# ScalarE's instructions ordered by the framework's scheduler instead of by the program

## The chip, the core and the metric

The kernel runs on one core of one Trainium2 chip, in one launch. The core has five engines, each with an instruction queue of its own: TensorE (PE in the profile; its weight loads are PEld), VectorE (DVE), ScalarE (ACT), GpSimd (POOL) and SyncE (SP), which here issues the transfers from and to the device's memory (HBM). The engines wait for one another by semaphores. The metric is the device time of the core in microseconds (us): 2713.55, the median of three runs (2711.83, 2713.55 and 2714.47).

## The reference

The computation is in float32 on one sequence of 512 tokens with 2048 channels. First come two hybrid attention layers:

```python
h = rms_norm(x, pre_w);  proj = h @ w_in                      # 2048 -> 5952
y_a = diff_attention(...)             # 4 heads, two softmaxes, their difference, causal
y_b = sliding_window_attention(...)   # 16 heads of 64, window 128, sinks
y_c = causal_attention(...)           # 4 heads; q and k, v from rms-normed latents of 512
y = concat(y_a, y_b, y_c) * silu(gates);  x = x + rms_norm(y @ w_out, post_w)
```

Then a second block: rmsnorm, a projection to mixer inputs and gates, of which 1024 channels go through a pooling mixer (trailing means over windows of 2, 4, 8 and 16 tokens, then a 256x256 map per group) and 1024 through a state space mixer (64 groups, 64 complex states each, a GLU behind), the gates, an output projection, a gated per-layer embedding and the norms around them.

## The kernel before

**Projections.** Each float32 operand is split in two float32r halves, and a product is three matmuls (`mm3`): high by high, low by high, high by low. The activations of a projection stand split in one big tile `B` (high and low halves of 16 k-tiles of 128 channels). Weights stream. SyncE loads a piece of up to 128x1024 into `wraw`, a ring of 3. For each unit of up to 128x512, ScalarE casts or scales it into `whi` (a ring of 6, `WBUFS`) and VectorE forms `wlo`, the rest; `split_unit` writes both, and `prefetch` has SyncE issue the next load once a `wlo` is written. `ahead` keeps 4 units split beside the one in use. A `whi` may be written only when its `wraw` has landed, and when TensorE and VectorE have used up the tile that had its place in the ring six units before. Results gather in PSUM banks: four of tag `pp`, two of `t`, one each of `s0` and `s1`. ScalarE and VectorE copy or combine them into tiles in SBUF (`raw`, `craw`, `o`, `gt`, `g`), which frees the bank.

**Norms.** `norm_list` takes a token tile of 128 rows through its steps: four squares with a sum (ScalarE, `junk<-x`), a reciprocal root in ten small VectorE instructions (`ry`), four scalings `h`, 16 transposes on TensorE into a bank, and `transpose_to_B`: a ScalarE cast to the high half of `B` and a VectorE subtraction for the low. `first_norm` does this at the start of the kernel for token tiles 0 and 1; ScalarE scales two of the `h` there. Tiles 2 and 3 are loaded then, too, but their steps run later, beside the first projection.

**Other work.** Attention, rotations, the pooling means, the state space scan and the gates are closures that run between the steps of the projections. `gate` has ScalarE write tanh of a bank to `g`, and VectorE multiply it in, which frees the bank. `split` is a ScalarE cast `hi` and a VectorE `lo`.

**What sets the order.** The program writes the instructions of all engines in one sequence, by a rough account of its own (`Model`, `chain`, `tick`) of when each engine would get to them. All are issued through one helper, so all rows of the profile carry its line, L166. `run` writes them inside a block that makes every engine keep the order in which they were written:

```python
        with self.tc.manual_schedule():
            self.first_norm(t["x"])
```

Each engine runs its queue in that order, and one that waits holds up all behind it. Slots of the tile pools are handed out as the program is laid out, in order.

Of the kernel before, what the change touches and what calls it, by code (L numbers as in the profile page):

```python
# [85 lines left out]
class Model:  # L86
    """A rough account, kept while the program is written, of when each engine gets to an instruction and
    each tile is written. Work beside the projections is placed where its operands should be there."""
# [53 lines left out]
    def ready(self, need, eng, banks):  # L142
        """Whether eng would find these tiles written and banks of these tags free."""
        limit = max(self.t[eng], self.t["PE"])
        for tag in set(banks):
            names, bufs = self.held.get(tag, ()), self.bufs.get(tag, 1)
            for i in range(len(names) + banks.count(tag) - bufs):
                if self.used.get(names[i], 0.0) + 130 > limit:
                    return False
        return all(x is not None and self.done.get(x.tensor.name, 1e18) + 130 <= limit for x in need)  # L150
# [5 lines left out]
class Engine:  # L156
    """An engine's instructions, passed on and entered in the model."""
# [24 lines left out]
class Step:  # L182
    """A piece of work that is best begun when eng would find the tiles that need() names written."""
# [9 lines left out]
class K:  # L193
# [87 lines left out]
    def chain(self, fs, gap=1.0, delay=0.0, q=None):  # L281
        """Steps that run one after another, at least gap ticks apart; None leaves a place free, and one
        that returns False is called again later."""
        self.n += 1
        heapq.heappush(self.bg if q is None else q, (self.now + delay + gap, self.n, list(fs), gap))

    def force(self, q):
        """Runs the next step that can be, ready or not."""
        self.run_urgent()
        late, got = [], False  # L290
        while q and not got:
            x = heapq.heappop(q)
            got = self.is_emitted(x[2][0]) and self.run_step(x[2][0]) is not False
            if got:
                self.advance(q, x)
            else:
                late.append(x)
        assert got
        for x in late:
            heapq.heappush(q, x)  # L300
# [17 lines left out]
    def att_start(self, units, ticks, delay=0, done=None):  # L318
        """Units of (scores, exp, norm, transposes, values); one is begun every so many ticks."""
        gap = ticks / len(units)  # L320
        t = self.now + delay
        for x in units:
            self.queue.append([list(x), 0, t])
            t += gap
        if done:
            self.queue[-1][0].append(done)

    def run_units(self, force=False):
        """A unit goes on once the one before it is two parts further."""
        before = 5  # L330
        for x in list(self.queue):
            steps, pos, t = x
            if t > self.now and not force:
                break
            while pos < len(steps) and (before >= min(pos + 2, 5)):
                f = steps[pos]
                if not (self.is_emitted(f) if force else self.is_ready(f)):
                    break
                self.run_step(f)
                pos += 1  # L340
                if force:
                    force = False
                    x[1] = pos
                    if pos == len(steps):
                        self.queue.remove(x)
                    return True
            x[1] = pos
            if pos == len(steps):
                self.queue.remove(x)
                before = 5  # L350
            else:
                before = pos
        return False
# [18 lines left out]
    def rsqrt_list(self, out, ss, scale, eps, n):  # L372
        """Closures that put (ss * scale + eps) ** -0.5 into out[0]."""
        nc = self.nc
        st = {}

        def first():
            mk = (lambda x: self.small(n, F32, x)) if n <= 8 else (lambda x: self.u(F32, [P, n], x))
            st["v"], st["y"], st["w"] = mk("rv"), mk("ry"), mk("rw")
            v, y = st["v"], st["y"]  # L380
            out.append(y)
            nc.vector.tensor_scalar(out=v, in0=ss, scalar1=scale, scalar2=eps, op0=ALU.mult, op1=ALU.add)
            nc.vector.tensor_scalar(out=y.bitcast(I32), in0=v.bitcast(I32), scalar1=-0.5, scalar2=1597463007.0,
                                    op0=ALU.mult, op1=ALU.add)

        def it():
            v, y, w = st["v"], st["y"], st["w"]
            nc.vector.scalar_tensor_tensor(out=w, in0=y, scalar=-0.5, in1=y, op0=ALU.mult, op1=ALU.mult)
            nc.vector.tensor_tensor(out=w, in0=w, in1=v, op=ALU.mult)
            nc.vector.scalar_tensor_tensor(out=y, in0=w, scalar=1.5, in1=y, op0=ALU.add, op1=ALU.mult)  # L390

        return [first, it, it, it]
# [7 lines left out]
    def rsqrt1(self, ss, scale, eps):  # L400
        """(ss * scale + eps) ** -0.5 of one column; the powers of two that the steps leave are taken out at the end."""
# [18 lines left out]
    def units(self, name):  # L420
        """How many units of up to 512 columns, and the k-tiles and columns of each."""
# [10 lines left out]
    def plan_loads(self):  # L432
        """Pieces of one or two units, and after which split the load of each is issued."""
# [55 lines left out]
    def ahead(self, n=AHEAD):  # L489
        """Keeps n units of the ring split beside the one in use."""  # L490
# [20 lines left out]
    def proj_cm(self, name, mov, ncol, evac, hook=None):  # L511
        """out[channel, token]: the weights stationary."""
# [17 lines left out]
    def proj_tm(self, name, stat, ms, evac, hook=None):  # L530
        """out[token, channel]: the activations stationary."""
# [99 lines left out]
    def reduce_list(self, tiles):  # L631
        """The steps of reduce_angle as closures."""
        return [lambda x=x: self.reduce_angle(*tiles(), part=x) for x in range(4)]

    def reduce_angle(self, a, k, r, part=None):
        """r = a - 2 pi round(a / 2 pi), the multiple taken off in pieces that are exact; in one go or by part."""
# [48 lines left out]
    def norm_list(self, m, xt, after_sq=None, tags="tttt", act=False, first=False):  # L685
        """Closures: x / rms(x), transposed into the columns of token tile m of B."""
# [72 lines left out]
    def rope_lists(self, raws, fins):  # L759
        """Rotates the [channel, token] tiles; fins get each result."""  # L760
# [29 lines left out]
    def to_stack(self, dst, i, keys=False):  # L790
        """Two heads of 64 rows for products whose 128 rows carry both parts: [hi; lo] and [lo; hi] of them, or,
        for keys, [hi; hi] of either, and the two heads' lo."""
# [14 lines left out]
    def mm_stacked(self, outs, qs, ks, rows, start=True):  # L807
        """hi hi + lo hi over 128 rows, then hi lo over the head's own 64."""
# [117 lines left out]
    def da_units(self, l, h, qk, va, done):  # L926
        """qk() gives the tiles of q and k; done(o) comes after the last one."""
# [3 lines left out]
        units = []  # L931
# [91 lines left out]
    def cm_norm_list(self, xs, n, eps, cols, after):  # L1023
        """Closures: x * rsqrt(mean over the channels) * column, for [channel, token] tiles, in place."""
# [60 lines left out]
    def plan_tail(self, name, last):  # L1085
        """The last chunk stays on the chip, split; the end of it stays in the ring."""
# [6 lines left out]
    def layer(self, l):  # L1093
# [66 lines left out]
        # sliding window  # L1160
# [44 lines left out]
        # differential attention  # L1205
# [47 lines left out]
        # latent attention, over the last projection and the first chunk of the output projection  # L1253
# [25 lines left out]
        def hook(k0):  # L1279
            """Rows of B that the last projection has passed take the branches' outputs."""  # L1280
# [27 lines left out]
    def tail_rows(self, name, evac):  # L1308
        """The resident last chunk, token tile by token tile."""
# [70 lines left out]
    def cmul(self, dst, a, b, e1, e2, tmp, neg_im=False):  # L1380
        """dst = a * b for (re, im) pairs of views; tmp: two scratch views."""
# [12 lines left out]
    def exp_list(self, get):  # L1394
        """exp of get() = (x, out, k, t), in closures; x, k and t are overwritten."""
# [157 lines left out]
    def cdiag(self, c, pr):  # L1553
        """c of two groups, each in its rows and columns."""
        return self.cd[c][pr // 16][:, pr % 16].rearrange("p e c -> p (e c)")

    def ssm_lists(self, ct, ud, yd, put):
        """Closures of one channel tile (8 groups): its tables, then the scan and its output."""
# [226 lines left out]
    def second(self, xsrc):  # L1785
# [36 lines left out]
        # pooling branch  # L1822
# [84 lines left out]
        # gated linear unit of the state space branch  # L1907
# [29 lines left out]
        # output projection, residual  # L1937
# [49 lines left out]
        # embedding, its gate, final norm  # L1987
# [56 lines left out]
    def run(self, upto=99):  # L2044
# [7 lines left out]
        with self.tc.manual_schedule():  # L2052
# [16 lines left out]
def _layout(inp):  # L2069
# [80 lines left out]
    # constants of the shapes  # L2150
# [35 lines left out]
```

## Time and profile before

| | |
|---|---|
| median of three runs | 2713.55 us (2711.83 to 2714.47) |
| span of the profiled execution, its own time in the profile | 2711.1 us |
| TensorE busy | 2648.9 us (98%) |
| VectorE busy | 1599.1 us (59%) |
| ScalarE busy | 1197.8 us (44%) |
| GpSimd busy | 415.5 us (15%) |
| mean granted TensorE clock | 0.993 of full speed |
| mean traffic of the DMA queues | 114 GB/s |

The profile is of one execution. Its page gives the busy time of each engine; a timeline gives for each instruction, or run of like instructions (x2, x4), the start, the time they took, what is written from what, and in brackets how long the engine had stood idle just before and what released it. Tiles go by the program's names with the buffer numbers left out. TensorE stands idle for 2711.1 - 2648.9 = 62.2 us in all. The largest pieces are 10.0 us before its first instruction and waits of up to 5.7 us for VectorE.

### The profile page before, as it was taken

The numbers are of one execution on the slowest core, as the hardware profiler recorded it, in microseconds if no ns is written. First come the engines' busy times: TensorE is split into PE (matmuls) and PEld (weight loads), VectorE is DVE, ScalarE is ACT, GpSimd is POOL, SyncE is SP. The second block draws the span as 40 slices with busy tenths as digits, with TensorE's granted clock in tenths as the row PEclk, the third lists the DMA queues.
The fourth block names the chain that finished last, engine by engine and source line by source line (L and its number), as shares of the span: only waits on it lengthen the run. The fifth ranks groups of instructions, "written<-read, shape, count | busy, mean of one in ns | idle before, by whom it ended". The sixth has DMA issues, their size and how long they took to land. (4 is left out here: it accounts for less than half of the span.)

```text
span 2711.1 us, 36803 instructions
## 1 busy us (share of the span) xinstructions
PE 2648.9 (98%) x13120; PEld 2201.1 (81%) x13120; DVE 1599.1 (59%) x3247; ACT 1197.8 (44%) x2543; POOL 415.5 (15%) x822
## 2 busy tenths in 40 slices
PE   8999999999999999999999999989999999999998
PEld 8978888877888887888777788888877888888886
DVE  6785566675624758546667562486767654333344
ACT  7565444544434646444444443463333343232341
POOL 0100001100001110000110000117777800000000
PEclk9999999999999999999999999999999999999999
DMA  6642333223235553224422323454232332352332
GB/s 213 186 120 86 91 119 113 75 78 125 71 116 163 173 147 94 94 89 122 117 71 79 124 70 117 160 186 141 84 94 82 100 99 94 118 164 69 101 127 91
DMA packets 125831, 309.04 MB, mean 114 GB/s; under 512 B 33616, under 2 KB 34512, under 8 KB 125648
## 3 DMA queue, kind: packets, MB, share of 16 engines
q1 hardware_dynamic: 125648, 306.69, 36.1%
q8 instruction: 103, 1.69, 0.3%
q14 instruction: 80, 0.66, 0.1%
HBM read 264.68 MB, written 20.97 MB: 105 GB/s over the span
## 5 line engine op out<-in xcount | busy, mean ns | idle before, releaser
L166 PE MATMUL pp<-B,whi 128*128 128x512 f32 (+1 forms) x4256 | 1222.6, 373 | 7.5 <-DVE g L166 6.2
L166 PEld LDWEIGHTS pp<-B,whi 128*128 128x128 f32 x4256 | 753.9, 190 | 137.7 <-issue 7.1
L166 PE MATMUL pp<-B,wlo 128*128 128x512 f32 (+1 forms) x2128 | 782.4, 368 | 8.9 <-DVE wlo L166 8.9
L166 PE MATMUL pp<-whi,B 128*128 128x512 f32 x1984 | 626.0, 391 | 1.6 <-ACT raw L166 1.0
L166 DVE SCALAR_TENSOR_TENSOR wlo<-wraw,p_cols,whi 128x512 fp32r<-128x512 f32 (+1 forms) x576 | 448.4, 795 | 293.7 <-ACT whi L166 290.0
L166 ACT ACTIVATE whi<-wraw,p_cols 128x512 fp32r<-128x512 f32 (+1 forms) x576 | 395.9, 713 | 206.8 <-PE pp L166 170.8
L166 PEld LDWEIGHTS pp<-B,wlo 128*128 128x128 f32 x2128 | 403.5, 190 | 78.2 <-DVE wlo L166 10.3
L166 PEld LDWEIGHTS pp<-whi,B 128*128 128x128 f32 x1984 | 372.4, 188 | 82.2 <-ACT raw L166 1.8
L166 DVE TENSOR_TENSOR wlo<-wraw,whi 128x512 fp32r<-128x512 f32 x288 | 197.8, 696 | 386.9 <-ACT whi L166 386.5
L166 PE MATMUL pp<-wlo,B 128*128 128x512 f32 x992 | 386.2, 389 | 0.0
L166 ACT CAST whi<-wraw 128x512 fp32r<-128x512 f32 x288 | 175.5, 623 | 323.4 <-PE pp L166 311.0
L166 PEld LDWEIGHTS pp<-wlo,B 128*128 128x128 f32 x992 | 186.4, 188 | 37.1
L166 POOL TENSOR_TENSOR sw<-sw,sinT 128x512 f32<-128x512 f32 x40 | 55.2, 1386 | 764.7 <-DMA sw<-raw 708.8
L166 POOL TENSOR_TENSOR o<-o,x 128x512 f32<-128x512 f32 x32 | 51.1, 1623 | 378.4 <-DVE o L166 370.4
L166 PE MATMUL pp<-rh,B 128*128 128x512 f32 x320 | 103.1, 392 | 0.0
L166 PE MATMUL pp<-hi,whi 128*128 128x512 f32 x224 | 88.3, 394 | 1.4 <-DVE lo L166 1.4
L166 PE MATMUL pp<-hi,wlo 128*128 128x512 f32 x224 | 87.3, 390 | 0.0
L166 PE MATMUL pp<-lo,whi 128*128 128x512 f32 x224 | 87.3, 390 | 0.0
L166 ACT ACTIVATE p<-p,nb 128x256 f32<-128x256 f32 (+1 forms) x128 | 60.2, 473 | 57.9 <-DVE nb L166 57.8
L166 ACT CAST pth<-t 128x256 fp32r<-128x256 f32 (+1 forms) x96 | 29.2, 339 | 113.2 <-PE t L166 110.5
L166 PEld LDWEIGHTS pp<-rh,B 128*128 128x128 f32 x320 | 60.1, 188 | 12.3
L166 DVE TENSOR_SCALAR p<-p,sm 128x128 f32<-128x128 f32 (+1 forms) x192 | 66.0, 386 | 4.1 <-DVE sm L166 0.5
(257 smaller groups left out, 3162.7 us busy)
## 6 DMA issues: line engine op xcount, KB each, us to landing
wraw<-in_w SPq DMA_DIRECT2D x426, 512.0 KB, 3.5
sw<-raw SPq DMA_DIRECT2D x160, 64.0 KB, 2.0
wraw<-in_w SPq DMA_DIRECT2D x24, 384.0 KB, 3.2
x<-in_x SPq DMA_DIRECT2D x32, 256.0 KB, 5.2
x<-o SPq DMA_DIRECT2D x32, 256.0 KB, 2.6
ybd<-yb SPq DMA_DIRECT2D x16, 256.0 KB, 4.5
yb<-ybd SPq DMA_DIRECT2D x16, 256.0 KB, 3.8
x<-x SPq DMA_DIRECT2D x16, 256.0 KB, 4.4
```

The costliest lines, as they stand in the source:

```text
L166: r = f(*a, **k)
```

## The change

The block that holds the order is given the engines that it is to hold: TensorE, SyncE, GpSimd and VectorE. ScalarE is no longer among them; its instructions are put in order by the framework's scheduler when the program is built, among those that its own account has ready. The rest of the diff blanks comments and docstrings:

```diff
@@ -140,7 +140,7 @@
     def ready(self, need, eng, banks):
-        """Whether eng would find these tiles written and banks of these tags free."""
+
...
@@ -2049,7 +2049,8 @@
             self.plan_layer(l)
         self.plan_second()
         self.plan_loads()
-        with self.tc.manual_schedule():
+        ordered = {mybir.EngineType.PE, mybir.EngineType.SP, mybir.EngineType.Pool, mybir.EngineType.DVE}
+        with self.tc.manual_schedule(engines=ordered):
             self.first_norm(t["x"])
```

In the built program the orders of TensorE, VectorE, GpSimd and SyncE are as before. On ScalarE the same compute instructions stand in another order over the whole program (2438 lines of difference for some 2080 rows); table loads are 5 in both. Three places follow; in each row stand the line, the operation, what is written from what, and the shape.

At the start of the program, ScalarE before: `x_102` is the last piece of token tile 1; `pp`, `s` and `t` are banks with transposes of token tiles 0 and 1; `h_215` and `h_217` are the two scalings that ScalarE has there.

```order
L166 ACTIVATE junk,s_146<-x_102 128x512
L166 CAST B<-pp_187 128x4x128
L166 CAST B<-pp_193 128x4x128
L166 CAST B<-pp_199 128x4x128
L166 CAST B<-pp_205 128x4x128
L166 ACTIVATE h_215<-x_101,ry_176 128x512
L166 ACTIVATE h_217<-x_102,ry_176 128x512
L166 ACTIVATE whi_223<-wraw_111,p_cols 128x384
L166 CAST B<-s_226 128x4x128
L166 CAST B<-s_234 128x4x128
L166 CAST B<-t_241 128x4x128
L166 CAST B<-t_248 128x4x128
```

The last square of tile 1 is followed by the casts of tile 0, and the two `h` before the first `whi`. On the same engine now, from the sixth `whi` of the program on (`x_107` to `x_110` are token tile 2, `x_121` to `x_124` token tile 3):

```order
L166 ACTIVATE whi_286<-wraw_115,p_cols 128x384
L166 ACTIVATE junk,s_330<-x_107 128x512
L166 ACTIVATE junk,s_330<-x_108 128x512
L166 ACTIVATE junk,s_330<-x_109 128x512
L166 ACTIVATE junk,s_330<-x_110 128x512
L166 ACTIVATE junk,s_623<-x_121 128x512
L166 ACTIVATE junk,s_623<-x_122 128x512
L166 ACTIVATE junk,s_623<-x_123 128x512
L166 ACTIVATE junk,s_623<-x_124 128x512
L166 CAST B<-pp_187 128x4x128
L166 CAST B<-pp_193 128x4x128
L166 CAST B<-pp_199 128x4x128
```

Six `whi` (five more stand before this piece) and the eight squares of tiles 2 and 3 now stand between the square of `x_102` and the casts; `h_215` follows the cast from `pp_199`, then the cast from `pp_205`, then `h_217`.

At the pooling gates of the second block (2116 to 2128 us in the profile), the difference on ScalarE, - before and + now. `mt` are copies for the state space mixer, `g` the tanh of four finished banks:

```order
-L166 CAST whi4240_20631<-wraw4207_20478 128x512
 L166 COPY mt4243_20653<-t4245_20655 128x4x64
 L166 COPY mt4244_20654<-t4245_20655 128x4x64
-L166 ACTIVATE whi4246_20662<-wraw4222_20546,p_cols_97 128x512
 L166 COPY mt4243_20653<-t4248_20678 128x4x64
 L166 COPY mt4244_20654<-t4248_20678 128x4x64
-L166 ACTIVATE whi4249_20685<-wraw4222_20546,p_cols_97 128x512
 L166 ACTIVATE g4251_20691<-pp4147_20141 128x512
 L166 ACTIVATE g4252_20697<-pp4148_20142 128x512
 L166 ACTIVATE g4256_20712<-pp4149_20143 128x512
 L166 ACTIVATE g4257_20718<-pp4150_20144 128x512
+L166 CAST whi4240_20631<-wraw4207_20478 128x512
```

The cast `whi4240` moved from ahead of the `mt` copies to behind the four `g`, and `whi4246` and `whi4249` follow it there. On VectorE the order is unchanged: the `wlo` of `whi4240`, two `lb`, two `ht`, the `wlo` of `whi4246`, then the first product with `g4251`.

In layer 0, at 333 us in the profile, the difference on ScalarE around two casts `hi` of softmax rows in banks `t`; `yb` are copies of attention outputs, `sa` and `sb` casts of rotated queries:

```order
+L166 ACTIVATE whi750_3659<-wraw712_3501,p_cols_97 128x512
+L166 ACTIVATE whi757_3696<-wraw712_3501,p_cols_97 128x512
+L166 ACTIVATE whi760_3717<-wraw727_3562,p_cols_97 128x512
 L166 CAST hi745_3648<-t744_3643 128x512
 L166 CAST hi748_3656<-t747_3651 128x512
-L166 ACTIVATE whi750_3659<-wraw712_3501,p_cols_97 128x512
 L166 COPY yb543_2638<-t752_3679 64x128 x2
 L166 COPY yb544_2639<-t752_3679 64x128 x2
 L166 CAST sa753_3691<-raw725_3554 128x512
 L166 CAST sb754_3692<-raw725_3554 64x512
-L166 ACTIVATE whi757_3696<-wraw712_3501,p_cols_97 128x512
-L166 ACTIVATE whi760_3717<-wraw727_3562,p_cols_97 128x512
```

Three `whi` moved ahead of the casts `hi745` and `hi748`; the first had stood just behind them, the other two behind the `yb`, `sa` and `sb`.

## Rows read from the trace of the kernel before

**Rows 1.** The page's head and its part 1: busy us, share of span, instructions

```profile
span 2711.1 us, 36803 instructions
PE 2648.9 (98%) x13120; PEld 2201.1 (81%) x13120; DVE 1599.1 (59%) x3247; ACT 1197.8 (44%) x2543; POOL 415.5 (15%) x822
```

**Rows 2.** Waits of ScalarE, VectorE, TensorE: us in total, times, longest

```profile
ACT whi L166 <- PE pp L166: 481.8, 281, 10.8
...
DVE wlo L166 <- ACT whi L166: 676.4, 373, 7.9
...
PE pp L166 <- DVE wlo L166: 8.9, 6, 2.4
...
PE t L166 <- DVE p L166: 5.0, 5, 1.8
```

**Rows 3.** SyncE's timeline at the start, and the loads issued from 7.4 us

```profile
7.44 6.70 SPq L166 DMA_DIRECT2D x<-in_x  x8
...
x<-in_x SPq DMA_DIRECT2D x8, 256.0 KB, 6.0
```

**Rows 4.** ScalarE's timeline, 11.5 to 30 us: start, us, instruction, [idle before]

```profile
11.96 1.54 ACT L166 CAST B<-pp 128x512 fp32r<-128x512 f32 x3
...
14.19 1.33 ACT L166 ACTIVATE h<-x,ry 128x512 f32<-128x512 f32 x2
...
25.28 0.62 ACT L166 ACTIVATE junk<-x 128x512 bf16<-128x512 f32 x1
...
26.02 0.63 ACT L166 ACTIVATE junk<-x 128x512 bf16<-128x512 f32 x1
```

**Rows 5.** TensorE's timeline at the start

```profile
16.50 1.92 PE L166 MATMUL t<-c_ident,h 128*128 128x128 f32 x8
18.06 1.17 PE L166 MATMUL pp<-B,whi 128*128 128x256 f32 x2
```

**Rows 6.** ScalarE's timeline at the pooling gate

```profile
2116.43 0.62 ACT L166 CAST whi<-wraw 128x512 fp32r<-128x512 f32 x1
...
2125.32 2.21 ACT L166 ACTIVATE g<-pp 128x512 f32<-128x512 f32 x4
```

**Rows 7.** VectorE's timeline at the pooling gate

```profile
2117.78 1.29 DVE L166 TENSOR_TENSOR lb<-lb,lbt 128x512 f32<-128x512 f32 x2
...
2122.26 0.75 DVE L166 SCALAR_TENSOR_TENSOR wlo<-wraw,p_cols,whi 128x512 fp32r<-128x512 f32 x1 [1.98 <-ACT whi L166]
2125.95 1.28 DVE L166 SCALAR_TENSOR_TENSOR g<-g,pp 128x512 f32<-128x512 f32 x2 [2.94 <-ACT g L166]
...
2132.67 1.24 DVE L166 SCALAR_TENSOR_TENSOR wlo<-wraw,p_cols,whi 128x512 fp32r<-128x512 f32 x1
```

**Rows 8.** TensorE's timeline at the pooling gate

```profile
2126.74 0.46 PE L166 MATMUL pp<-hi,whi 128*128 128x512 f32 x1
```

**Rows 9.** Timelines: ScalarE at 333, TensorE at 336, ScalarE at 1750 us

```profile
332.98 1.08 ACT L166 CAST hi<-t 128x512 fp32r<-128x512 f32 x2 [3.20 <-PE t L166]
...
335.96 0.39 PE L166 MATMUL t<-hi,v 128*128 128x512 f32 x1
...
1749.65 2.56 ACT L166 ACTIVATE h<-o,ry 128x512 f32<-128x512 f32 x4 [0.90 <-DVE ry L166]
```

**Rows 10.** Timelines: GpSimd at 1944, VectorE at 1946, TensorE at 2004 us

```profile
1944.20 1.19 POOL L166 TENSOR_TENSOR pw<-pv 128x511 f32<-128x511 f32 x1 [2.43 <-ACT hi L166]
...
1946.05 0.69 DVE L166 SCALAR_TENSOR_TENSOR pw<-pw,pv 128x512 f32<-128x512 f32 x1
...
2003.74 1.22 PE L166 MATMUL pp<-B,whi 128*128 128x512 f32 x2 [5.71 <-DVE g L166]
```

**Rows 11.** Timelines around 540 us: TensorE, VectorE

```profile
544.90 0.66 PE L166 MATMUL t<-c_ident,p 128*128 128x128 f32 x4 [1.68 <-DVE p L166]
...
540.00 1.28 DVE L166 SCALAR_TENSOR_TENSOR wlo<-wraw,p_cols,whi 128x512 fp32r<-128x512 f32 x1 [2.12 <-ACT whi L166]
```

**Rows 12.** A stretch: us, busy of five engines (PE, PEld, ...), granted clock, DMA

```profile
2002.30:2009.10 6.80, 5.36 (x21) 4.98 (x22) 6.25 (x13) 0.00 (x0) 3.08 (x3) 0.50 0.28 85
```

## The prediction

> **What bounds the kernel now.** I read the page first, then the waits of three engines, then the timelines of the places where ScalarE's order changes. TensorE is busy 2648.9 of 2711.1 us, ScalarE 44% [rows 1]. So the time is TensorE's work and some 62 us in which it stands still, and a new order on ScalarE can only move those 62 us, or add to them. ScalarE has much idle time, and the reason is the ring of weights: 281 times, 481.8 us in all, a `whi` is the next instruction and waits until TensorE has used a tile of the ring up; VectorE in turn stands 676.4 us waiting for `whi` before it can make `wlo` [rows 2]. TensorE waits little for the outcome, 8.9 us for `wlo` and 5.0 us for the softmax rows `p` [rows 2]. A reader should take two things from this. A `whi` that may not start yet is the usual state of ScalarE's queue, so whatever stands behind one waits for TensorE; and a `whi` earlier by some us gives VectorE its idle time back, which matters where VectorE is late.
>
> The profiled execution has no other time than its span, 2711.1 us, which is 2.45 us (0.09%) below the median of the runs, 2713.55. I sum changes of the span and add 2.45.
>
> **The change, part by part.** No instruction is added, removed or resized, and the program order of TensorE, VectorE, GpSimd and SyncE stays. ScalarE's instructions are the same; where they stand is new. The cost is therefore found place by place: does an instruction that TensorE needs now stand behind one that becomes ready later?
>
> *Start.* Before, ScalarE begins the 4 `B` casts at 11.96 us, the two `h` of 0.66 us each at 14.19 [rows 4]. Now six `whi` and the eight squares of token tiles 2 and 3 stand ahead of them, as the first two fences of the change show. Those squares need x tiles that are not there yet: SyncE issues the eight loads from 7.44 to 14.14 us, so the last begins at about 13.3, and a load takes 6.0 us to land [rows 3]; that is 19.3 to 20.1. The last square takes 0.74 more (25.28 to 26.02 is one with its sum [rows 4]). So the first cast goes at 20.0 to 20.9 instead of 11.96. Behind it come three casts (1.54 us), `h`, a cast (0.51) and `h`: the second `h` ends at 23.4 to 24.3. TensorE needs it for four transposes (8 take from 16.50 to 18.06, 0.2 us each) and then begins the first projection [rows 5]: 24.2 to 25.1 instead of 18.06. That is +6.1 to +7.0; I take **+6.6**. VectorE cannot help, since its halves of `B` follow the casts one by one. The six `whi` cost nothing here, they run while the loads are still on their way. In what ScalarE no longer does later there is no gain, since it idles there.
>
> *The pooling gate.* Before, the `whi` of 2116.43 us stood well ahead of the four tanh `g` of 2125.32 [rows 6]. Now it and two more stand behind all four (third fence), and those are tied to TensorE: the last `g` ends at 2127.53. `whi` is then ready at about 2128.1, eleven us late. VectorE keeps its order and stops at the `wlo` of that unit, which stands ahead of `lb` at 2117.78; behind that `wlo` (0.67) are two `lb` and two `ht` (1.22 each pair), then the `wlo` of 2122.26 (0.67), and only then `g`, which before began at 2125.95 [rows 7]. So 2128.1 + 0.6 + 2.4 + 0.7 = 2131.8, and the first `g` frees its bank at 2132.4. TensorE began the next product in that bank at 2126.74, without idle time [rows 8]. It stands until 2132.5: **+5.8**. Bounds: not under 3, as the `whi`, the `wlo` and the `g` alone are that long; at most 5.8 and four VectorE instructions stretched like the `wlo` of 2132.67, which took 1.24 in place of 0.75 us beside GpSimd [rows 7], so 7.8.
> The Trainium skill (SBUF — State Buffer, "Who interferes with whom") says that a VectorE instruction with two SBUF inputs and a GpSimd instruction that reads SBUF exclude each other, one fully waiting. By that rule the four `lb` and `ht` would each wait for a GpSimd instruction and the place would cost about 8; the rows are divided, the 1.24 agrees and the `lb` of 0.65 each do not, and I stay with the rows.
>
> *A cast or scaling behind a `whi` that must wait.* At 332.98 us two `hi` casts feed TensorE's `t<-hi,v` at 335.96 [rows 9]. Now two `whi` that were far behind stand ahead (fourth fence); the second needs the ring's tile that TensorE gives back as it ends the unit before 335.96. So `hi` starts after 336.0 + 0.7, the first product waits until 337.3, and `lo` comes later still: **+2.0**. Its twin in layer 1 costs **+1.6** by the same count. At the ends of both layers one square (0.74) or one `whi` (0.6) is put ahead of the `h` scalings that TensorE's transposes follow directly, as at 1749.65 [rows 9]; six such places at about 0.8 make **+4.8**. Five more before 170 us, `raw` copies and `B` casts behind a `whi`, I put at **+3.4** together. The four add to 11.8; nothing if `whi` turns out to be ready each time, 18 if waits pile up.
>
> *GpSimd.* Tiles are handed out in another order, and GpSimd's `pw` at 1944.20 now gets its tile only when VectorE has ended the `pw` of 1946.05, at 1946.74. GpSimd could go no earlier than 1944.2 before, so it is 2.5 us late and works without a pause to the place where TensorE waits 5.71 us, at 2003.74 [rows 10]; 0.6 of it has room. **+1.9**, between 0 and 2.5.
>
> *Gains.* At 544.90 TensorE waits 1.68 us for `p`, and VectorE had stood 2.12 us before 540.00 for a `whi` that ScalarE made late [rows 11]. With `whi` ahead the `wlo` falls into that idle time, and the gap closes, 1.7 here and in its twin. Eight smaller gaps of this kind give 0.2 to 1.0 each, 3.7 together. Sum **-7.1**, at most the 13.9 us that TensorE waits for `wlo` and `p` [rows 2].
>
> *Clock.* Around the wait that ends at 2003.74 the granted clock is 0.50 (1.2 instead of 2.4 GHz) for 6.8 us, with 5.36 us of work in them [rows 12]; that work would take half as long at full clock, so such a wait costs 2.7 us more than itself. I add **+2.7** at the pooling gate, where the new idle time is as long (0 to 3.4), and **+2.0** at the start, where the clock had just risen (0 to 3.4).
>
> Sum: 6.6 + 5.8 + 11.8 + 1.9 + 4.7 - 7.1 = +23.7. Span 2734.8, time **2737 us**.
>
> **The rivals.** (a) *Earlier `whi` wins.* The scheduler's preference for `whi` feeds VectorE earlier everywhere, and the small places cost nothing since `whi` is ready in time. For it: VectorE's 676 us of waiting [rows 2]. Price: the start with its clock (+8.6) against -13.9: 2708 us. It decides where the gain passes the start's 8.6, so only if the pooling gate, too, is hidden. Against it: `g` there has no room, TensorE followed it without idle time [rows 8]. Chance 0.07, faster in most of it.
>
> (b) *It makes no difference that can be measured* (within 0.2%, 5.4 us): ScalarE is 44% busy and TensorE runs ahead, the places that I count have more room than I see, only start and gate remain partly and the gains pay them: 6.6 + 3 - 7.1 = +2.5, 2716 us. Against it: the start's loads land when they land. The Trainium skill (Trace Analysis, "Identifying Performance Opportunities") has improvement come from the most-contended engine; by it an order on an engine at 44% would be near this case. Chance 0.10.
>
> (c) *Waits pile up.* Each place that stops TensorE shifts the rest, the clock halves at several more of them, and VectorE and GpSimd meet. Upper ends: 7.0 + 7.8 + 18 + 2.5 + 6.8 - 4 = +38, 2752 us; with what I have not seen in some hundred further moved `whi`, 2765. Chance 0.13.
>
> (d) The forecast, the sum of places within 2720 to 2750: 0.70.
>
> The range goes from 2717 (part of b) to 2756 (most of c). Faster takes most of (a), 0.06; within 0.2% takes (b) and the rest of (a), 0.11; slower takes (c) and (d), 0.83. A change of 0.2% is about what a measurement of this kernel tells from none.
>
> **What would show it.** In the profile after: the first `CAST B<-pp` near 21 us instead of 11.96, behind squares; the first projection near 24.7. Around 2132 us a wait of TensorE of 5 to 8 us on VectorE's `g` that was not there, with a stretch of half clock behind it. `hi` behind `whi` near 340 and TensorE waiting for `hi` or `lo`. No wait for `p` near 551. TensorE's busy time grows by no more than the half clock makes of it. The prediction is wrong if the first projection begins before 20 us, if no new wait over 3 us stands at the gate, or if TensorE's total wait falls.

## The result and the profile after

The changed kernel takes 2730.7 us (median of four runs, 2727.2 to 2732.2) against 2712.7 us for the kernel before (four runs, 2708.2 to 2714.5): ratio 1.0066, 95% interval 1.0054 to 1.0078. It is slower by 18 us; 2737 were forecast.

The page's head of the kernel after:

```profile
span 2727.9 us, 36907 instructions
PE 2650.2 (97%) x13120; PEld 2201.5 (81%) x13120; DVE 1581.5 (58%) x3247; ACT 1218.5 (45%) x2543; POOL 419.2 (15%) x822
```

TensorE's busy time grew by 1.3 us only, and the span by 16.8 [rows 1]. So the loss is standing still. TensorE's waits that changed most, first in the kernel before, then in the kernel after, and behind them the two waits of the ring (us in total, times, longest):

```profile
PE pp L166 <- DVE g L166: 6.2, 2, 5.7
...
PE s L166 <- DVE ys L166: 4.7, 1, 4.7
PE t L166 <- ACT h L166: 3.3, 3, 2.2
```

```profile
PE t L166 <- ACT h L166: 14.8, 7, 7.6
PE pp L166 <- DVE g L166: 12.6, 3, 6.5
...
PE pp L166 <- DVE wlo L166: 7.7, 7, 2.3
PE pp L166 <- ACT raw L166: 6.5, 7, 3.0
...
PE t L166 <- DVE p L166: 2.2, 4, 0.8
...
PE s L166 <- DVE ys L166: 0.7, 1, 0.7
...
ACT whi L166 <- PE pp L166: 837.4, 492, 10.8
...
DVE wlo L166 <- ACT whi L166: 527.0, 295, 7.5
```

The wait of VectorE for `whi` fell from 676.4 to 527.0 us, that of ScalarE for TensorE rose from 481.8 to 837.4 [rows 2]: ScalarE makes `whi` as early as the ring lets it, and stands in front of the next one, with whatever is behind it. The price is in TensorE's waits for `h` (14.8 instead of 3.3, of which 7.6 at the start) and for `g` (12.6 instead of 6.2); the gain is in `p`, 2.2 instead of 5.0 [rows 2], and in `ys`, 0.7 instead of 4.7.

Since TensorE runs the same instructions in the same order, the start of each can be subtracted, after minus before; where that difference steps, a place costs or gives. The steps, worked out so from the two traces, in the order of the prediction's terms (a step holds the wait and what a lower clock takes behind it):

| place (us in the kernel before) | forecast | measured step |
|---|---|---|
| start, 16 to 21 | +6.6 and +2.0 | +6.65 |
| pooling gate, 2127 | +5.8 and +2.7 | +7.5 |
| `hi` at 336 and its twin at 1216 | +2.0, +1.6 | +3.9, +1.65 |
| six layer-end places, 883 to 1812 | +4.8 | +9.8 (926: 4.4, 1805: 2.7) |
| five places before 170 | +3.4 | +6.2 (135 to 141: 4.1) |
| GpSimd's `pw`, felt at 2004 | +1.9 | -0.1 |
| gains for `p` and the like (489, 545, 760, 1078, 1370, 1424, 2607) | -7.1 | -8.5 |
| losses not foreseen (406, 419, 983, 1029) | | +3.1 |
| gains not foreseen (910, 1050, 1507, 1782 to 1797, 2103) | | -13.6 |

A trace is of one execution, and some steps come and go between traces whose order at the place is the same: 1.6 us where a lower clock follows a wait or does not (138, 336, 627, 1507, 1791), up to 2.5 us at the start, and at places behind a load 3.5 to 4.4 us (926) and 1.0 to 4.6 us (1805). So the table is good to a few us in a row with such a place.

**The start** [rows 4, 5]. ScalarE, then TensorE, in the kernel after:

```profile
11.82 3.14 ACT L166 ACTIVATE whi<-wraw,p_cols 128x384 fp32r<-128x384 f32 x6 [0.18 <-DMA wraw<-in_w]
14.87 0.61 ACT L166 ACTIVATE junk<-x 128x512 bf16<-128x512 f32 x1
...
20.19 0.63 ACT L166 ACTIVATE junk<-x 128x512 bf16<-128x512 f32 x1
...
20.82 1.54 ACT L166 CAST B<-pp 128x512 fp32r<-128x512 f32 x3
...
23.33 0.75 ACT L166 ACTIVATE h<-x,ry 128x512 f32<-128x512 f32 x1
...
23.03 2.21 PE L166 MATMUL t<-c_ident,h 128*128 128x128 f32 x8 [7.62 <-ACT h L166]
24.90 1.05 PE L166 MATMUL pp<-B,whi 128*128 128x256 f32 x2
```

The six `whi` run from 11.82, the eight squares from 14.87, one every 0.75 us, the last at 20.19, and the first cast goes at 20.82 instead of 11.96. The second `h` is begun at 23.33, and the first projection starts at 24.90 instead of 18.06; 20.0 to 20.9, 23.4 to 24.3 (its end) and 24.2 to 25.1 were forecast.

The times are those forecast, the reason is another. By the trace the eight x tiles land between 14.34 and 19.49 us, each ahead of its square: only the second square stands for its tile, 0.09 us, and the last begins 0.7 us after its own has landed. What fills the stretch is ScalarE's own work, 9.0 us from the first `whi` to the first cast. In the traces of three of the experiments below (e2, e7 and e8), with the same order at the start, it is 8.9 us, and no square waits.

**The pooling gate** [rows 6 to 8]. ScalarE, VectorE and TensorE in the kernel after:

```profile
2135.59 2.67 ACT L166 ACTIVATE g<-pp 128x512 f32<-128x512 f32 x4
2138.16 0.61 ACT L166 CAST whi<-wraw 128x512 fp32r<-128x512 f32 x1
...
2138.80 0.69 DVE L166 TENSOR_TENSOR wlo<-wraw,whi 128x512 fp32r<-128x512 f32 x1 [7.55 <-ACT whi L166]
2139.41 1.29 DVE L166 TENSOR_TENSOR lb<-lb,lbt 128x512 f32<-128x512 f32 x2
...
2142.49 1.27 DVE L166 SCALAR_TENSOR_TENSOR g<-g,pp 128x512 f32<-128x512 f32 x2
...
2143.21 0.79 PE L166 MATMUL pp<-hi,whi 128*128 128x512 f32 x1 [5.59 <-DVE g L166]
```

The stretch behind it (columns as in rows 12):

```profile
2143.20:2147.00 3.80, 3.79 (x11) 3.10 (x12) 3.26 (x6) 0.00 (x0) 3.72 (x8) 0.50 0.40 132
```

The `whi` follows the four `g` at 2138.16, VectorE had stood 7.55 us for it, `g` is begun at 2142.49, and TensorE, which before did not wait here, stands 5.59 us (5.8 forecast). Behind that it has 0.50 of its clock. The four `lb` and `ht` between are not stretched (1.29 for two).

**`hi` behind `whi`** [rows 9]. ScalarE and TensorE in the kernel after, then the stretch behind:

```profile
349.29 0.72 ACT L166 ACTIVATE whi<-wraw,p_cols 128x512 fp32r<-128x512 f32 x1 [2.88 <-PE pp L166]
349.92 1.05 ACT L166 CAST hi<-t 128x512 fp32r<-128x512 f32 x2
...
351.26 0.53 PE L166 MATMUL t<-hi,v 128*128 128x512 f32 x1 [2.06 <-DVE lo L166]
```

```profile
352.00:356.00 4.00, 4.00 (x13) 3.13 (x12) 2.38 (x4) 1.96 (x6) 0.25 (x1) 0.62 0.08 34
```

Both `hi` are cast at 349.92, at once behind the `whi` that had waited for TensorE, and TensorE waits 2.06 us for `lo`, where 2.0 were forecast. Not forecast: the granted clock is 0.62 on average in the 4 us behind, which is most of the other 1.9 us of the step.

**A load that has not landed.** At the largest of the layer-end places the `whi` waits for something else. ScalarE and TensorE in the kernel after (926 us in the kernel before):

```profile
937.33 0.72 ACT L166 ACTIVATE whi<-wraw,p_cols 128x512 fp32r<-128x512 f32 x1 [3.32 <-DMA wraw<-in_w]
937.96 0.57 ACT L166 CAST B<-t 128x512 fp32r<-128x512 f32 x1
...
941.84 0.92 ACT L166 COPY raw<-pp 128x256 f32<-128x256 f32 x3
...
942.26 0.80 PE L166 MATMUL pp<-B,whi 128*128 128x256 f32 x2 [3.01 <-ACT raw L166]
```

A `whi` stands 3.32 us for its `wraw`, with a cast of `B` and the `raw` copies behind it, and TensorE waits 3.01 us for `raw` to free a bank. I had counted `whi` that wait for TensorE, 0.8 us a place; a load can be later than that. How late differs from run to run: this load took 7.3 us from issue to landing, in the trace of the experiment e1 (same order here) 5.7 us, and TensorE's wait was 2.0 there.

**The gains** [rows 11]. VectorE and TensorE at the place of the wait for `p` in the kernel after:

```profile
554.58 1.41 DVE L166 SCALAR_TENSOR_TENSOR wlo<-wraw,p_cols,whi 128x512 fp32r<-128x512 f32 x2
...
560.56 0.60 PE L166 MATMUL t<-c_ident,p 128*128 128x128 f32 x4
```

The two `wlo` begin at 554.58, some 3 us earlier against TensorE than at 540.00 before, in the time in which VectorE used to stand for `whi`; `p` comes before TensorE needs it, and TensorE's transposes have no idle time in front.

**The largest unforeseen gain** is at 2103 us. VectorE, GpSimd and TensorE there in the kernel before, then the same instructions in the kernel after:

```profile
2096.45 5.06 DVE L166 TENSOR_TENSOR sp<-sx,z 64x252 f32<-64x252 f32 x4
...
2097.70 2.35 POOL L166 TENSOR_TENSOR lbt<-pk,sbb 128x512 f32<-128x512 f32 x2
...
2102.97 1.20 PE L166 MATMUL s<-sp,ht 128*128 128x128 f32 x4 [4.67 <-DVE ys L166]
```

```profile
2111.05 2.54 DVE L166 TENSOR_TENSOR sp<-sx,z 64x252 f32<-64x252 f32 x4
...
2113.68 3.12 POOL L166 TENSOR_TENSOR lbt<-pk,sbb 128x512 f32<-128x512 f32 x2 [1.32 <-DVE sp L166]
...
2115.07 0.68 PE L166 MATMUL s<-sp,ht 128*128 128x128 f32 x4 [0.71 <-DVE ys L166]
```

Before, four `sp` took 5.06 us, the first beside GpSimd's `pw`, the others beside its `lbt`, and TensorE waited 4.67 us for the `ys` behind them. After, GpSimd waits for `sp` before it begins `lbt`: in the program the wait for the slot that the tile of `lbt` is given is now for VectorE, where it was for TensorE. The four `sp` take 2.54 us (1.25 of them the first, again beside `pw`) and TensorE waits 0.71. A new order on ScalarE changed when tiles come free, with that the slots that later tiles get, and with that whom GpSimd waits for.

### The profile page after: what moved, and what is told of

Its sections match the earlier page's. It is cut to its first block, busy times and chain, and to the rows that moved or that the text cites. A ratio compares the mean times of both kernels' runs of the same rounds, so it can differ in the third digit from the quotient of the medians.

```text
span 2727.9 us, 36907 instructions
## 1 busy us (share of the span) xinstructions
PE 2650.2 (97%) x13120; PEld 2201.5 (81%) x13120; DVE 1581.5 (58%) x3247; ACT 1218.5 (45%) x2543; POOL 419.2 (15%) x822
## 3 DMA queue, kind: packets, MB, share of 16 engines
q8 instruction: 103, 1.69, 0.3%
## 5 line engine op out<-in xcount | busy, mean ns | idle before, releaser
L166 ACT ACTIVATE whi<-wraw,p_cols 128x512 fp32r<-128x512 f32 (+1 forms) x576 | 406.8, 714 | 552.4 <-PE pp L166 436.8
L166 DVE TENSOR_TENSOR p<-s,c_mask 128x512 f32<-128x512 f32 (+1 forms) x64 | 39.5, 618 | 69.8 <-PE s L166 69.7
L166 DVE TENSOR_TENSOR s<-s,c_mask 128x128 f32<-128x128 f32 x96 | 28.3, 295 | 72.3 <-PE s L166 72.1
```

The source lines that it names most:

```text
L166: r = f(*a, **k)
```

## The experiments

There are eight, e1 to e8. In all but e4, ScalarE's order is the program's in some stretches and the scheduler's in the others; a stretch is named by weight units, counted by `split_unit`. All other engines keep the program's order. With no free stretch this gives the order of the kernel before, with one over the whole program that of the kernel after. The edit to the kernel after, for the first:

```diff
         def call(*a, **k):
-            r = f(*a, **k)
+            r = f(*a, **k); model.keep(name, r)
...
+    FREE = ((12, 10000),)
+
+    def keep(self, eng, r):
+        if eng != "ACT":
+            return
+        free = any(a <= self.n_split < b for a, b in self.FREE)
+        for x in self.tail if free else self.tail + self.loose:
+            self.tc.add_manual_dep(r.ins, x.name, self.NOSYNC)
+        if free:
+            self.loose.append(r.ins)
+        else:
+            self.tail, self.loose = [r.ins], []
```

The kernel before ran beside all of them (2712.7 us beside the first four, 2713.1 beside the last four).

**Start kept, e1** (the edit above).

> ScalarE keeps the program's order up to the twelfth weight unit (about the first 35 us) and is left to the scheduler from there on; nothing else differs from the kernel after. Theory (the time is the sum of places, each place its own): the first B cast goes back to 12 us, the first projection to 18.1, and the raw copy behind a whi at 38 us is undone too: 6.65 + 1.0 us less than the kernel after, about 2723 us, ratio 1.004 to the kernel before. Rival (the loss is spread over the whole program, by the many semaphore waits that ScalarE's new order brings): under 2 us of gain, 2729 or more. Rival (what is saved at the start is lost again at the next wait): 2728 to 2731.

Measured: 2721.2 us, ratio 1.0035 (1.0022 to 1.0047), 9.5 us under the kernel after. The first casts are back at 11.29 us, ScalarE and TensorE of this run:

```profile
11.29 0.59 ACT L166 CAST B<-pp 128x512 fp32r<-128x512 f32 x1
...
16.70 0.38 PE L166 MATMUL pp<-B,whi 128*128 128x256 f32 x1 [0.19 <-ACT B L166]
```

Against the kernel after the steps are -7.7 at the start, and smaller ones later (-1.5 behind the waits at 135 to 141, -1.0 at 926, -1.2 at 983, +1.6 at 1507). The place theory holds for the start; what is saved is not lost again, and there is no spread loss. That 7.7 is what was expected for two places is chance: the `raw` copy at 38 us is not undone, TensorE still waits 0.97 us for it and the step of +1.0 against the kernel before stands, and the start came out 1.0 us earlier than in the trace of the kernel before, with the same order.

**Gate kept, e2.**

```diff
-    FREE = ((12, 10000),)
+    FREE = ((0, 698), (714, 10000))
```

> ScalarE keeps the program's order for 16 weight units around the pooling gate (2090 to 2160 us) and is left to the scheduler elsewhere. Theory (places): the wait of TensorE for g at the gate (6.5 us in the kernel after) and its stretch of half clock go, 7.5 us less than the kernel after: about 2723 us, ratio 1.004. The wait for ys 25 us before, which had shrunk to 0.7, stays small. Rival (VectorE and GpSimd are the bound there, the gate only shows it): the wait moves on to the next product, gain under 3 us, 2728 or more.

Measured: 2722.0 us, ratio 1.0033 (1.0021 to 1.0046). TensorE at the gate has no idle time in front of the product again:

```profile
2135.47 0.44 PE L166 MATMUL pp<-hi,whi 128*128 128x512 f32 x1
```

The step there is -7.56 us against the kernel after, and the wait for `ys` stays small. The rest of the 8.7 us by which it is under the kernel after lies at places where the order is the same and the steps vary (-1.5 at 138 and -1.6 at 336, where the clock did not fall this time, +1.6 at 1507). The wait was not a bound of VectorE or GpSimd: it did not move on.

**Only the stretches with gains free, e3.**

```diff
-    FREE = ((12, 10000),)
+    FREE = ((170, 318), (374, 415), (426, 570), (608, 700), (712, 10000))
```

> ScalarE is left to the scheduler only in those stretches in which TensorE lost less idle time in the kernel after than before (about 447 to 915 us, 1045 to 1190, 1225 to 1695, 1812 to 2095, 2145 to the end); it keeps the program's order in the others, the start and the gate among them. Theory (places, and the gains do not hang on the losses ahead of them): the gains alone stay, 5.0 + 2.4 + 4.0 + 5.5 + 1.1 = 18 us less than the kernel before, about 2695 us, ratio 0.9935. Rival (the gains only make up for delays that the losses made): about as before, 2710 to 2715. Rival (spread loss by waits): over 2715.

Measured: 2700.3 us, ratio 0.9952 (0.994 to 0.9965): faster than both kernels, by 12.4 us where 18 were expected. TensorE's waits in this run:

```profile
PE pp L166 <- ACT raw L166: 2.6, 3, 1.6
...
PE t L166 <- DVE p L166: 1.1, 2, 0.7
```

`p` costs 1.1 instead of 5.0 us. The gains at 489, 545, 760, 910, 1370, 1424, 2103 and 2607 are there to 0.1 us. Those at 1050 and 1507 are not (3 us): the one makes up for losses just ahead (it is there in e7, where only the stretch ahead of it is free), the other was the clock's. And some losses stay, 1.6 at 926 behind the end of a free stretch and 0.4 at 883; the start, in the program's order, came out 1.0 later in this run. So the larger gains stand on their own.

**GpSimd waits for `sp`, e4**, in the kernel before:

```diff
-            G.tensor_tensor(out=tmp[0], in0=a[1], in1=b[1], op=ALU.mult)
+            g = G.tensor_tensor(out=tmp[0], in0=a[1], in1=b[1], op=ALU.mult)
+            if ct == 6:
+                self.tc.add_manual_dep(g.ins, self.last_sp.ins.name, mybir.DependencyInfo(
+                    mybir.DependencyClass.Sync, mybir.DependencyReason.DATA))
```

> The kernel before, with the program's order on all engines, and one wait added: GpSimd's first lbt of the seventh channel tile (2097.7 us) waits until VectorE has ended the four sp of the sixth, as a tile slot makes it wait in the kernel after. Theory (the wait of TensorE for ys at 2103 us went because VectorE's sp no longer runs beside GpSimd's lbt, 0.41 us each instead of 1.25): the four sp take 2.5 instead of 5.1 us, TensorE's wait falls from 4.7 to about 1 us and its half clock goes: 2707 to 2709 us, ratio 0.998. Rival (the wait went because whi and wlo are earlier there): sp shortens but the wait stays at 3 us or more, no gain, or a loss of up to 2 us by the later lbt.

Measured: 2709.2 us, ratio 0.9989 (0.998 to 0.9998). VectorE, GpSimd and TensorE of this run:

```profile
2096.92 1.69 DVE L166 TENSOR_TENSOR sp<-sx,z 64x252 f32<-64x252 f32 x4
...
2098.76 3.05 POOL L166 TENSOR_TENSOR lbt<-pk,sbb 128x512 f32<-128x512 f32 x2 [2.39 <-DVE sp L166]
...
2100.08 0.68 PE L166 MATMUL s<-sp,ht 128*128 128x128 f32 x4 [2.17 <-DVE ys L166]
```

The four `sp` take 1.69 us, and TensorE's wait falls from 4.67 to 2.17, where about 1 was expected: 2.5 us by the wait alone, 3.3 with the clock behind it, of the 5.3 that the kernel after gains there. The theory holds for the larger part. The other part is, I take it, VectorE, which reaches `sp` 1.6 us earlier against TensorE in the kernel after, where `whi` is earlier; that was not tried by itself.

**Gains trimmed, e5.**

```diff
-    FREE = ((170, 318), (374, 415), (426, 570), (608, 700), (712, 10000))
+    FREE = ((170, 306), (374, 415), (426, 500), (608, 700), (712, 10000))
```

> As e3, but three of the free stretches are cut: the second ends before the layer end (at about 870 instead of 915 us), the fourth at 1480 instead of 1695 us, so that no cast or scaling at a layer end and none at 926 us stands behind a whi. Theory (places): the small losses of e3 at 883 and 926 us (0.4 and 1.6) go, and with them the gain at 910 (1.8) that it had there; the rest is as in e3: 2699 to 2702 us. Rival (gains that come later hang on a head start that VectorE collects over a long free stretch): 2704 or more.

Measured: 2698.5 us, ratio 0.9948 (0.9935 to 0.996), the fastest kernel here, though not clear of e3's interval. Two stretches are shorter than in e3, the first and the third. The steps of the gains are as in e3 except at 910, where the gain went as expected; that at 926 is 0.6, that at 883 stayed at 0.4. The larger gains, that at 2103 among them, need no long free stretch.

**Only the `whi` ahead at the start, e6.**

```diff
-    FREE = ((12, 10000),)
+    FREE = ((0, 7),)
```

> The kernel before, except that ScalarE has the six whi of the start ahead of the first casts (as in the kernel after), with the eight squares where the program has them. Tells apart what the squares and the six whi cost at the start. Theory (the squares' wait for the x loads makes the cost): the casts start behind the whi at 15.0 instead of 20.8 us, the first projection at 19 to 20 instead of 24.9: 1 to 2 us more than the kernel before, 2714 to 2715, ratio 1.0005. Rival (the whi cost as much as the squares): projection after 21.5 us, 2716 or more.

Measured: 2712.6 us, ratio 1.0003 (0.9994 to 1.0012), no difference that can be told. ScalarE and TensorE:

```profile
12.80 3.14 ACT L166 ACTIVATE whi<-wraw,p_cols 128x384 fp32r<-128x384 f32 x6
15.85 1.53 ACT L166 CAST B<-pp 128x512 fp32r<-128x512 f32 x3
...
19.91 1.04 PE L166 MATMUL pp<-B,whi 128*128 128x256 f32 x2
```

The casts follow the six `whi` at 15.85 and the projection starts at 19.91, 5.0 us earlier than in the kernel after. So of the 6.84 us by which it starts later there, the squares make some three quarters, and by their length, since they wait 0.09 us in all for loads there. What the six `whi` cost is not shown. The step at the start is +2.4, but a piece of x landed late in this run (the `whi` begin at 12.80, in the kernel after at 11.82), and in e5, whose order at the start is that of the kernel before, the step is +2.5. In this trace the -1.6 at 1507 and -2.1 at 1791 hide it, and the interval of the times, some 2.4 us to either side, is too wide to tell it.

**Only the stretches with losses free, e7.**

```diff
-    FREE = ((12, 10000),)
+    FREE = ((0, 170), (318, 374), (415, 426), (570, 608), (700, 712))
```

> The complement of e3: ScalarE is left to the scheduler only where TensorE lost idle time in the kernel after (the start to about 447 us, 915 to 1045, 1190 to 1225, 1695 to 1812, 2095 to 2145), and keeps the program's order in between. Theory (places add up): the kernel after is before + losses - gains; gains alone were 12.5 us in e3, the sum is 18, so the losses alone are some 30.5: about 2743 us, ratio 1.011. Rival (places do not add up, a delay is used up as slack by the next place): 2735 or less.

Measured: 2743.1 us, ratio 1.011 (1.0094 to 1.0125), 2743 expected. The totals add up: with e3's 12.4 us of gain and these 30 us of loss the change's 18 are accounted for. Single places do not all keep their size: 926 steps by 0.5 here (4.4 in the kernel after), 1805 by 5.5 (2.7), 2103 by +1.7, and the gate by 10.1 (7.5), in a trace that is of the slowest of the four runs. TensorE at the gate:

```profile
2158.27 0.79 PE L166 MATMUL pp<-hi,whi 128*128 128x512 f32 x1 [7.34 <-DVE g L166]
```

**The rotations of layer 0 kept, e8.**

```diff
-    FREE = ((12, 10000),)
+    FREE = ((0, 64), (88, 10000))
```

> The kernel after, with ScalarE in the program's order between about 97 and 165 us (the rotations of layer 0, where a cast of v stands behind three whi that wait for TensorE) and left to the scheduler elsewhere. Theory (places): the waits for wlo at 135 to 141 us and the one at 155 go, 4.1 + 0.7 us, about 2726 us, ratio 1.005. Rival (the head of the program leaves VectorE late, and the waits there come from the start's delay of 6.7 us): gain under 2 us.

Measured: 2726.9 us, ratio 1.0055 (1.0042 to 1.0067). The steps against the kernel after are -4.1 at 135 to 141 and -0.7 at 155; in the profiled run later steps (+1.6 at 1507, +1.9 at 1805, +0.7 at 2004) give most of it back. The places theory holds, the waits there did not come from the late start.

## Why the prediction was right, and where it was not

- **The bound and the way to count**: right. TensorE's busy time changed by 1.3 us only, and the time is a sum of places whose totals add up, as e3 and e7 show from both sides, though single places differ by some us between runs.
- **Start**: the time was right (24.90 in 24.2 to 25.1) and the place, as e1 shows, but not the reason. The prediction has the squares stand for their loads, the last to land setting the time, with the `whi` for nothing. In the trace the last tile lands at 19.49, which by that sum puts the first cast at 20.2; it went at 20.82, since 9.0 us of `whi` and squares run back to back. Two sums of nearly the same length stood side by side, and that they met is luck. The squares could not have run much earlier without the `whi`, as the first two tiles land at 14.34 and 15.59. The 2.0 us for the clock were too much: the step with everything in it is 6.65.
- **Gate**: right in its mechanism and size, 5.59 us of wait and a half clock behind; e2 takes it out.
- **Casts behind a `whi`**: the mechanism was right, the size was not: 11.8 forecast, about 21.5 measured, and 3.1 at places that I had not listed. Two things were missing. One is the load: at 926 and 1805 the `whi` in front waited for its `wraw`, where I had priced only waits for TensorE. The other is the clock, which I added at two places; it also fell behind the waits at 141, 336, 926 and 1766. Both vary: in e2's trace, with the same order at these places, the clock did not fall at 141 and 336, and 1805 cost 1.0 instead of 2.7, so that some 5 of the 21.5 us are this execution's.
- **GpSimd's `pw`**: wrong. GpSimd was late by 1.9 there (2.5 forecast), but 1.2 of that was made up on the way, and the wait at 2004 grew only by 0.8:

```profile
2020.69 1.22 PE L166 MATMUL pp<-B,whi 128*128 128x512 f32 x2 [6.48 <-DVE g L166]
```

  Behind it the clock came back earlier. I had treated GpSimd's work as of fixed length; beside VectorE it is not (the `pw` on 128x510 took 1.49 us before and 1.03 after).
- **Slots**: I looked at the new slots only for a wait that costs. The same cause gave the largest single gain, 5.3 us at 2103, by a wait that keeps GpSimd and VectorE apart.
- **Gains by earlier `whi`**: right, 8.5 for 7.1 at the places named.
- **The total**: 23.7 forecast, 16.8 between the two traces. Casts and losses not listed were 13 us too little; the clock at start and gate and GpSimd's `pw` 5 too much; gains of 15 us not seen or too small, of which some 3 (at 1507 and in 1782 to 1797) are clock steps that do not come again in e1 and e2. The direction was right for the reasons given, the size by some luck, since errors of 13 and 20 us met.
- **Rivals**: (a) fell, the gains alone are 12.4 us and not more than the losses; (b) fell: the order of an engine that is 44% busy cost 0.66%, with an interval clear of 0.2%. The Trainium skill (Perfetto Trace Analysis, "Identifying Performance Opportunities") says that improving a kernel generally means improving the most-contended engine. It does not speak for (b), as I had it do: TensorE, 97% busy, is that engine here, and ScalarE's order counts by making it wait. (c) fell in its sum, 2752, though the clock did fall at four more places.

## What to carry to other kernels

An in-order engine with idle time is not free: what counts is whether an instruction that the bounding engine needs stands behind one that becomes ready later, by a ring, a load or a bank, and how long what stands ahead of it takes by itself. Such places can be named from the trace of before and added up; the price of one was good to 2 us at the start and the gate, and too low by half where the clock or a load came in. Leave the order to a scheduler where nothing that is waited for can get behind a prefetch, and keep it by hand at starts, at layer ends and where a bank must come free: here a mix, its stretches chosen from the two traces, is 0.5% faster than the one and 1.2% faster than the other (2698.5 against 2712.7 and 2730.7 us). And look at what a new order does to tile slots, since they decide who waits for whom on other engines.

## What the runs showed of the hardware

- The same wait of TensorE does not always cost the same clock. Behind the wait of 2.2 us that ends at 1507 us the granted clock was 0.50 for 3.4 us in the kernel before and 1.00 in the kernel after, where the same wait was 2.15 us:

```profile
1507.40:1510.80 3.40, 3.40 (x9) 2.62 (x9) 2.71 (x5) 1.30 (x3) 0.00 (x0) 0.50 0.20 41
```

```profile
1523.60:1527.00 3.40, 3.40 (x15) 2.81 (x16) 2.71 (x5) 1.63 (x3) 0.00 (x0) 1.00 0.10 28
```

  That is 1.6 us in the steps, up or down, in several of the runs. Behind the wait of 2.06 us at 336 it is the same: 0.55 over the 3.4 us behind it in the kernel after, 1.00 in e2, with the same order. Such steps are a part of the spread of the times (2708.6 to 2714.7 us in the 15 runs of the kernel before beside the last four experiments), and a difference of 2 us is better told from a trace, place by place.
- VectorE and GpSimd hold each other up, and which of them pays is a matter of who came first. Four `sp` took 5.06 us beside `pw` and `lbt` and 1.69 alone; by their single rows the `lbt` began at 2097.70 and 2098.78, the `sp` beside them at 2097.71 and 2099.10. At the gate it was GpSimd: six `rx` on 128x4 took 3.29 us, all but the first 0.53 to 0.72 instead of 0.21 each, while VectorE did `lb` and `ht` without a stretch, each `lb` and `ht` begun 0.1 to 0.2 us ahead of an `rx`:

```profile
2138.68 3.29 POOL L166 TENSOR_TENSOR rx<-rx 128x4 f32<-128x4 f32 x6
```

  The Trainium skill (SBUF — State Buffer, "Who interferes with whom") has it so: two SBUF inputs on VectorE and a GpSimd instruction that reads SBUF exclude each other, and the order of issue decides which one stands. Both cases agree; in the prediction I had looked for the stretch on VectorE's side only.
